# Fourier–Hyena encoder layer: later sines and tables in the opening, and part of the odd weights' and of token 512's arithmetic given to GpSimd

## The chip, the cores and the metric

The kernel runs on one core of a Trainium2 chip. The metric is the device time of one execution in microseconds (us), of which lower is better. The engines of the core are named as the profile names them: PE is TensorE's matmul, PEld its weight load, DVE is VectorE, ACT is ScalarE, POOL is GpSimd, and SP is SyncE, which here issues most of the DMA transfers. Each engine works through a queue of its own, in order; an instruction whose operands are not there yet holds up everything behind it on that engine.

## The reference

The layer is applied to two sequences of 1024 tokens and 1024 channels (`x_prompt` and `x_sample`). The Fourier branch, on which the change works, is the part below; the Hyena branch (long convolutions with filters that a small sine network makes), the gates and the output projection follow the same normalised input.

```python
def encoder_layer(x, g_pre, w_in, ...):
    xn = rmsnorm(x, g_pre)
    p = xn @ w_in
    fv, fg, hv, hg, mg = jnp.split(p, ...)
    fz = fv.astype(jnp.float32).reshape(B, L, F_GROUPS, F_GROUP_DIM)
    fz = jnp.fft.fftn(fz, axes=(1, 3), norm="ortho").real
    y_f = (fz * jax.nn.silu(fg)) @ w_fourier_out
...
def hyena_filters(L, w1, b1, f1, w2, b2, f2, w3, decay):
...
    h = jnp.sin(f1 * (z @ w1 + b1))
    h = jnp.sin(f2 * (h @ w2 + b2))
    h = (h @ w3).reshape(L, N_DIR, H_ORDER, H_WIDTH)
```

Everything is in float32. The kernel keeps that accuracy by splitting an operand into a rounded high part and the rest (`split`: a cast, then a subtraction of the cast from the source), and multiplying the parts separately.

## The kernel before

The program begins with `phase_fourier`, which runs the Fourier branch for the prompt (b = 0) and then for the sample (b = 1). The filter network, the projections, the convolutions and the output follow. The change touches the first 61 us, the opening of the prompt, before TensorE's work becomes continuous. In the opening these steps are written down in this order:

- `hidden(0)` (L271): the filter network's first layer. Two matmuls into `phd` (L295), then `sin_of` (L258 to L269) reduces the argument on DVE, and the nested function `sines` takes the sine on ACT (L301, with a table load of its own) and stores `d_h1` (L302). The result lies in the tile `hd_0`, which takes a buffer of the ring `eo`. `sines` is called so that it stands behind the last square of `norm` on ACT.
- `norm(0)` (L306): eight loads of x, 512 KB each (L320), a square with sum on ACT for each (L323), and for each four of them a chain of 11 small DVE operations (`rstd`, L241 to L252), which gives `rs`, and four diagonal matrices `dg` (L328).
- For each k of the eight channel blocks, `weights(..., k, True)` (L363) and `xtile(0, k, ...)` (L331). `weights` loads a block of the Fourier columns of the projection into `wfv` (L367, 260 KB, two buffers) and forms their even part (`wer`, an addition) and their odd part (`wor`, a subtraction), with two buffers each. Each is then split into a rounded part by ACT (`we0`, `wo0`, L171) and a second part (`we1`, `wo1`, L181). `xtile` transposes and normalises x by matmuls with `dg` into PSUM (`tpx`, L194, two buffers `T`), copies it out on ACT in two halves (`xg`, L347, two buffers), stores it to `d_x` on SP (L348), and forms sums and differences of mirrored tokens (`eo`, DVE, 2 of 128x512). These are split into `eh` (ACT, L171) and `el` (DVE, L181). Token 512 is split separately into `x5` (a cast, L173, and a subtraction, L181, of 128x2).
- For each k the matmuls `pfv` (L194) add up products of `eh`, `el` with `we`, `wo` for the first half of the columns. They are the last thing before `fourier_half`, whose first matmuls (`pse`) read the table `seq`.
- Constant tables: `seq` (2064 KB), `alt` (86 KB), `chan` (384 KB) and `chx` (256 KB) are loaded through POOL's queue (L538 to L541). Two small casts on POOL (L537) that read `rs` hold `seq` and `chan` back until the norm is done; `alt` and `chx` wait for nothing.

The instructions are written stage by stage, and a scheduler decides ahead of the run in which order each engine's queue holds them. `tc.issue_after(i)` keeps what is written under it behind instruction i in that order. A ring of two buffers (`xg`, `wfv`, `wer`, `wor`, `T`) means that round k+2 waits until all readers of round k are done; for `xg` the store to `d_x` is one of these readers. The second half of the columns (the call of `weights` with `first` False) has its odd part and its second part on POOL already.

Of the kernel before, what the change touches and what calls it, by code (L numbers as in the profile page):

```python
# [9 lines left out]
F32 = mybir.dt.float32  # L10
# [6 lines left out]
P = 128  # L17
D = 1024
L = 1024
# [142 lines left out]
class K:  # L162
# [5 lines left out]
    def split(self, h, l, src, eng="pool", heng="act"):  # L168
        nc = self.nc
        if heng == "act":  # L170
            self.rounded = nc.scalar.copy(h, src)  # L171
        else:
            nc.vector.tensor_copy(h, src)  # L173
        self.left = self.sub(eng, l, src, h)
# [96 lines left out]
    def hidden(self, layer, px, pf):  # L271

        nc, a = self.nc, self.a
        h = px.tile([P, L], F32, tag="eo", name=f"hd_{layer}", bufs=2)
        out = [h[:, 0:512], h[:, 512:1024]]
        z = px.tile([P, L], F32, tag="x", name="hd_z", bufs=3)
        if layer == 0:
# [5 lines left out]
            w, z = w[0:33], z[0:33]  # L283
            y, k = [[pf.tile([P, 512], F32, tag=f"{t}p{n}", name=f"s{t}", bufs=1 + (t == "p")) for n in range(2)]
                    for t in "qp"]
        else:
# [12 lines left out]
        def sines():  # L299
            for n in range(2):  # L300
                nc.scalar.activation(out[n], y[n], AF.Sin)  # L301
            nc.sync.dma_start(self.d_h if layer else self.d_h1, h)  # L302
        return sines
# [26 lines left out]
    def xtile(self, b, k, px, fo):  # L330
# [11 lines left out]
        for n in range(2):  # L342
# [4 lines left out]
            nc.scalar.activation(xg[:, 512 * n:512 * n + 512], tp, AF.Copy, scale=self.gpre[:, k:k + 1])  # L347
        nc.sync.dma_start(self.d_x[b][k], xg[:, 0:L])  # L348
        eo = px.tile([P, 2, 2, 256], F32, tag="eo", name="eo", bufs=2)
# [5 lines left out]
        x5 = fo["x5"][:, k]  # L355
        self.split(x5[:, b:b + 33:32], x5[:, 2 + b:35 + b:32], xg[:, 512:513].to_broadcast([P, 2]), "dve", "dve")

# [5 lines left out]
    def weights(self, pw, W, half, k, first):  # L363
# [6 lines left out]
        self.add("dve", we, w[:, :, 0], w[:, :, 1])  # L370
        self.sub("dve" if first else "pool", wo, w[:, :, 0, 0:128], w[:, :, 1, 0:128])
        for r, t in ((we, W[0]), (wo, W[1])):
            self.split(t[0][:, k], t[1][:, k], r.rearrange("p a b -> p (a b)"), "pool" if r is wo and not first else "dve", "act")

# [114 lines left out]
    def phase_fourier(self):  # L489
        tc, nc, a = self.tc, self.nc, self.a  # L490
        with ExitStack() as es:
# [5 lines left out]
            fo = {}  # L497
# [13 lines left out]
            for b in range(NB):  # L511
                fo["eh"] = pe.tile([P, 8, 2, 2, 256], F32R, tag="eh", name="eh")
                fo["el"] = pe.tile([P, 8, 2, 2, 256], F32R, tag="el", name="el")
                if b == 0:
                    sines = self.hidden(0, px, pf)
                with tc.issue_after(behind.ins) if b else ExitStack():
                    self.norm(b, px, pf)
                if b == 0:
                    with tc.issue_after(self.squared.ins):
                        sines()  # L520
                begun = {}
# [4 lines left out]
                for k in range(8):  # L526
                    if b == 0:
                        with tc.issue_after(self.scaled.ins):
                            self.weights(pw, W, 0, k, True)
                    self.xtile(b, k, px, fo)  # L530
                    for (e, m), p in begun.items():
                        self.pfv(p, e, m, k, W, fo)
                for half in ((0, 1), (1, 0))[b]:
                    if b + half == 0:
                        nc.sync.dma_start(self.vec, a["c_vec"])
                        for t in ("seq", "chan"):
                            nc.gpsimd.tensor_copy(fo[t][:, 0, 0:1], self.rs[:, 7:8])  # L537
                        nc.gpsimd.dma_start(fo["seq"], a["c_seq"])  # L538
                        nc.gpsimd.dma_start(fo["alt"], a["c_alt"])
                        nc.gpsimd.dma_start(fo["chan"], a["c_chan"])  # L540
                        nc.gpsimd.dma_start(fo["chx"].rearrange("p a b c -> p (a b c)"), a["c_chx"])  # L541
                    elif b + half != 2:
# [982 lines left out]
```

## Time and profile before

| | us |
|---|---|
| median of 3 runs | 2418.81 (2416.72 to 2419.53) |
| the profiled execution | 2420.15 |
| its span in the trace | 2418.3 |
| first transposes begin on PE | 16.19 |
| first `pfv` matmul begins | 27.65 |
| first `pse` matmul begins (end of the opening) | 60.83 |

All times in the trace count from the start of the span. The views used below are the page of the whole run, the list of waits (which engine's instruction stood idle, for which producer, in total, how often, and the longest), tables of busy time by stretch of time, the timeline (start, duration, engine, line, operation), and the lists for single lines and groups, which give the duration of one instruction and the time that a DMA transfer took from its issue to its landing. Of the DVE's work in the opening, the 16 `wor` and `wo` operations took 0.42 us each, and the casts and subtractions of `x5` mostly 0.16 us each.

### The profile page before, as it was taken

What the parts mean: (1) busy time and instruction counts of PE and PEld (TensorE: products, weight loads), DVE (VectorE), ACT (ScalarE), POOL (GpSimd) and SP (SyncE); (2) the same over time, 40 slices, a digit from 0 to 9 for tenths busy, and PEclk for the clock granted to TensorE, in tenths of its full rate; (3) what the DMA queues carried; (4) which work ended last, traced back from release to release, by engine and by line L of the source; (5) the groups of instructions that cost most, each with busy time, mean ns of one, the idle gap of its engine ahead of it and who ended that gap; (6) DMA issues with size and microseconds to landing.
All of it is one profiled execution on the core that took longest, in us unless ns stands there. A gap on an engine that the chain in (4) does not pass through costs nothing. (4 is left out here: it accounts for less than half of the span.)

```text
span 2418.3 us, 37119 instructions
## 1 busy us (share of the span) xinstructions
PE 2360.6 (98%) x13006; PEld 2050.7 (85%) x13006; DVE 1976.0 (82%) x3760; ACT 1147.7 (47%) x2140; POOL 447.5 (19%) x575
## 2 busy tenths in 40 slices
PE   6999899999999999999999999999999999999998
PEld 6998788888888888888888888888878888888886
DVE  7786888888737999899899999997666687777787
ACT  6546666666544444344222322333344475656543
POOL 1331111111123332221023454310000000101000
PEclk9999899999999999999999999999999999999999
DMA  7536688787778777666365666553546687888754
GB/s 277 187 127 220 179 222 222 202 225 215 202 219 254 221 223 209 192 177 200 126 194 191 210 218 205 187 179 123 205 158 230 210 298 256 267 270 230 222 159 154
DMA packets 265010, 499.63 MB, mean 207 GB/s; under 512 B 26662, under 2 KB 92423, under 8 KB 264568
## 3 DMA queue, kind: packets, MB, share of 16 engines
q1 hardware_dynamic: 220076, 380.53, 48.0%
q0 software_dynamic: 44560, 116.72, 19.0%
q8 instruction: 102, 1.67, 0.3%
q14 instruction: 84, 0.69, 0.1%
q10 hardware_dynamic: 188, 0.02, 0.0%
HBM read 333.59 MB, written 167.77 MB: 207 GB/s over the span
## 5 line engine op out<-in xcount | busy, mean ns | idle before, releaser
L194 PE MATMUL pin<-xh,wh 128*128 128x512 f32 x1024 | 401.2, 393 | 0.4 <-DMA wh<-d_w 0.4
L194 PE MATMUL pin<-xl,wh 128*128 128x512 f32 x1024 | 401.2, 392 | 0.0
L194 PE MATMUL pin<-xh,wl 128*128 128x512 f32 x1024 | 399.6, 392 | 0.0
L194 PE MATMUL pin<-xh,whl 128*128 128x512 f32 x896 | 292.4, 397 | 8.1 <-DMA whl<-in_w_in 4.5
L194 PEld LDWEIGHTS pin<-xh,wh 128*128 128x128 f32 x1024 | 192.8, 188 | 35.9 <-DMA wh<-d_w 0.8
L194 PEld LDWEIGHTS pin<-xh,wl 128*128 128x128 f32 x1024 | 192.7, 188 | 35.6 <-DMA wl<-in_w_in 0.2
L194 PEld LDWEIGHTS pin<-xl,wh 128*128 128x128 f32 x1024 | 192.7, 188 | 34.8
L194 PEld LDWEIGHTS pin<-xh,whl 128*128 128x128 f32 x896 | 168.3, 190 | 42.8 <-DMA whl<-in_w_in 5.2
L194 PE MATMUL pT<-cinv,yh 128*128 128x256 f32 x1024 | 192.9, 283 | 2.7 <-ACT yh L171 2.7
L194 PE MATMUL pin<-xl,whl 128*128 128x512 f32 x448 | 178.1, 398 | 0.0
L194 PEld LDWEIGHTS pT<-cinv,yh 128*128 128x128 f32 x1024 | 165.4, 191 | 12.9 <-ACT yh L171 3.2
L194 PE MATMUL pX<-bh,cfwd 128*128 128x256 f32 x768 | 159.3, 287 | 0.9 <-ACT bh L171 0.9
L181 DVE TENSOR_TENSOR t<-pX,k 128x1024 f32<-128x1024 f32 x128 | 155.7, 1216 | 3.9 <-PE pX L194 2.9
L171 ACT CAST yh<-y 128x512 fp32r<-128x512 f32 x128 | 79.3, 620 | 152.8 <-DVE y L181 113.1
L194 PE MATMUL pT<-cinv,yl 128*128 128x256 f32 x512 | 145.5, 284 | 0.0
L171 ACT CAST bh<-b 128x512 fp32r<-128x512 f32 x144 | 88.9, 619 | 98.3 <-DVE b L181 58.1
L194 PEld LDWEIGHTS pX<-bh,cfwd 128*128 128x128 f32 x768 | 125.8, 191 | 4.6 <-ACT bh L171 1.3
L181 POOL TENSOR_TENSOR draw<-draw 128x256 f32<-128x256 f32 x96 | 93.8, 977 | 112.1 <-DMA draw<-in_w_out 39.5
L181 DVE TENSOR_TENSOR bl<-b,bh 128x512 fp32r<-128x512 f32 x144 | 100.3, 703 | 11.5 <-ACT bh L171 11.4
L194 PE MATMUL pX<-bl,cfwd 128*128 128x256 f32 x384 | 109.5, 285 | 0.0
L181 DVE TENSOR_TENSOR yl<-y,yh 128x512 fp32r<-128x512 f32 x128 | 90.2, 705 | 16.9 <-ACT yh L171 16.5
L194 PEld LDWEIGHTS pT<-cinv,yl 128*128 128x128 f32 x512 | 98.2, 192 | 1.9
(368 smaller groups left out, 6030.0 us busy)
## 6 DMA issues: line engine op xcount, KB each, us to landing
k<-d_k SPq DMA_DIRECT2D x128, 512.0 KB, 4.6
wr<-in_w_in SPq DMA_DIRECT2D x136, 256.0 KB, 3.6
d_g<-gt SPq DMA_DIRECT2D x92, 256.0 KB, 3.3
d_k<-kt SPq DMA_DIRECT2D x128, 128.0 KB, 3.7
d_k<-kt SPq DMA_DIRECT2D x64, 256.0 KB, 3.6
fz<-d_g SPq DMA_DIRECT2D x64, 256.0 KB, 5.1
wl<-in_w_in POOLq DMA_DIRECT2D x56, 256.0 KB, 5.4
whl<-in_w_in POOLq DMA_DIRECT2D x56, 256.0 KB, 5.7
```

Of the source, the lines that this page charges most:

```text
L171: self.rounded = nc.scalar.copy(h, src)
L181: return e.tensor_tensor(out, a, b, op=op)
L194: return self.nc.tensor.matmul(out, lhsT, rhs, start=start, stop=stop, skip_group_check=shared)
```

## The change

Six things change, all of them in the opening of the prompt:

1. `split` can have its cast done by POOL. The `x5` parts of the prompt, 8 casts and 8 subtractions of 128x2, go from DVE to POOL.
2. The odd weight part `wor` and the second part `wo1` of the first half, 16 operations of 128x256, go from DVE to POOL.
3. `sines` of the first layer is called behind the `eh` cast of k = 2, instead of behind the last square. Its result lies in buffers of its own (a third set of the tag `p`) instead of a buffer of the ring `eo`.
4. `d_h1` is stored in two halves of 64 rows (128 KB each), where 128 rows were stored at once (512 KB). Only these 64 rows are read later.
5. The tables are loaded later. `seq` is divided into the columns of its two halves. The first half and `alt` are held back by a POOL cast that reads `el` of k = 3, the second half by one that reads `el` of k = 4, `chan` and `chx` by one that reads `el` of k = 5.
6. The first loads of x for the sample are issued behind the store of `d_x` for k = 4 as well.

```diff
@@ split
-            nc.vector.tensor_copy(h, src)
+            (nc.vector if heng == "dve" else nc.gpsimd).tensor_copy(h, src)
@@ hidden
-        h = px.tile([P, L], F32, tag="eo", name=f"hd_{layer}", bufs=2)
-        out = [h[:, 0:512], h[:, 512:1024]]
+        if layer:
+            h = px.tile([P, L], F32, tag="eo", name=f"hd_{layer}", bufs=2)
+            out = [h[:, 0:512], h[:, 512:1024]]
...
-            y, k = [[pf.tile([P, 512], F32, tag=f"{t}p{n}", name=f"s{t}", bufs=1 + (t == "p")) for n in range(2)]
-                    for t in "qp"]
+            y, k, out = [[pf.tile([P, 512], F32, tag=f"{t}p{n}", name=f"s{t}", bufs=1 + (t == "p")) for n in range(2)]
+                         for t in "qpp"]
...
                 nc.scalar.activation(out[n], y[n], AF.Sin)
-            nc.sync.dma_start(self.d_h if layer else self.d_h1, h)
+                if layer == 0:
+                    nc.sync.dma_start(self.d_h1[64:128, 512 * n:512 * n + 512], out[n][64:128])
+            if layer:
+                nc.sync.dma_start(self.d_h, h)
@@ xtile
-        self.split(x5[:, b:b + 33:32], x5[:, 2 + b:35 + b:32], xg[:, 512:513].to_broadcast([P, 2]), "dve", "dve")
+        mid = xg[:, 512:513].to_broadcast([P, 2])
+        self.split(x5[:, b:b + 33:32], x5[:, 2 + b:35 + b:32], mid, "dve" if b else "pool", "dve" if b else "pool")
@@ weights
-        self.sub("dve" if first else "pool", wo, w[:, :, 0, 0:128], w[:, :, 1, 0:128])
+        self.sub("pool", wo, w[:, :, 0, 0:128], w[:, :, 1, 0:128])
         for r, t in ((we, W[0]), (wo, W[1])):
-            self.split(t[0][:, k], t[1][:, k], r.rearrange("p a b -> p (a b)"), "pool" if r is wo and not first else "dve", "act")
+            self.split(t[0][:, k], t[1][:, k], r.rearrange("p a b -> p (a b)"), "pool" if r is wo else "dve", "act")
@@ phase_fourier
-                with tc.issue_after(behind.ins) if b else ExitStack():
+                with tc.issue_after(behind.ins) if b else ExitStack(), tc.issue_after(stored.ins) if b else ExitStack():
                     self.norm(b, px, pf)
-                if b == 0:
-                    with tc.issue_after(self.squared.ins):
-                        sines()
...
                     self.xtile(b, k, px, fo)
+                    if b == 0 and k == 2:
+                        with tc.issue_after(self.rounded.ins):
+                            sines()
+                    if b == 0 and k == 4:
+                        stored = self.stored
...
-                        for t in ("seq", "chan"):
-                            nc.gpsimd.tensor_copy(fo[t][:, 0, 0:1], self.rs[:, 7:8])
-                        nc.gpsimd.dma_start(fo["seq"], a["c_seq"])
-                        nc.gpsimd.dma_start(fo["alt"], a["c_alt"])
-                        nc.gpsimd.dma_start(fo["chan"], a["c_chan"])
-                        nc.gpsimd.dma_start(fo["chx"].rearrange("p a b c -> p (a b c)"), a["c_chx"])
+                        chx = fo["chx"].rearrange("p a b c -> p (a b c)")
+                        tables = [(3, fo["seq"][:, :, 0:1032], a["c_seq"][:, :, 0:1032]), (3, fo["alt"], a["c_alt"]),
+                                  (4, fo["seq"][:, :, 1032:2064], a["c_seq"][:, :, 1032:2064]),
+                                  (5, fo["chan"], a["c_chan"]), (5, chx, a["c_chx"])]
+                        for k, t, src in tables:
+                            nc.gpsimd.tensor_copy(t[:, 0, 0:1] if len(t.shape) > 2 else t[:, 0:1],
+                                                  fo["el"].bitcast(F32)[:, k, 0, 0, 0:1])
+                            nc.gpsimd.dma_start(t, src)
```

Three queues show what moves. Numbers at the ends of names tell the buffers of one ring apart; `xg0_1` is b = 0, k = 1.

The first is ACT's queue right behind the eighth square. Before it read:

```order
L301 ACT_TABLE_LOAD
L301 ACTIVATE hd_0_296<-sq_303 128x512
L301 ACTIVATE hd_0_296<-sq_304 128x512
L347 ACTIVATE xg0_0_417<-tpx_419,gpre_66 128x512
L171 CAST we0_397<-wer_409 128x260
L171 CAST wo0_399<-wor_410 128x256
L171 CAST we0_397<-wer_459 128x260
L171 CAST wo0_399<-wor_460 128x256
L347 ACTIVATE xg0_1_467<-tpx_469,gpre_66 128x512
L347 ACTIVATE xg0_0_417<-tpx_425,gpre_66 128x512
L347 ACTIVATE xg0_1_467<-tpx_475,gpre_66 128x512
L171 CAST eh_294<-eo_432 128x1024
```

The same place of the changed kernel, from the cast of the first odd weights (k = 0) to the first `eh`:

```order
L171 CAST wo0_397<-wor_408 128x256
L351 ACTIVATE xg0_0_415<-tpx_417,gpre_66 128x512
L171 CAST wo0_397<-wor_458 128x256
L171 CAST we0_395<-wer_407 128x260
L171 CAST we0_395<-wer_457 128x260
L351 ACTIVATE xg0_1_465<-tpx_467,gpre_66 128x512
L171 CAST we0_395<-wer_507 128x260
L171 CAST wo0_397<-wor_508 128x256
L351 ACTIVATE xg0_0_415<-tpx_423,gpre_66 128x512
L171 CAST we0_395<-wer_561 128x260
L171 CAST wo0_397<-wor_562 128x256
L351 ACTIVATE xg0_1_465<-tpx_473,gpre_66 128x512
```

The sines are gone from here, and the casts for k = 2 (`wer_507`, `wor_508`) and k = 3 (`wer_561`, `wor_562`) now stand ahead of the second halves of `xg` of k = 0 and k = 1.

The second is POOL's queue behind the two small loads at the program's start. Before:

```order
L539 DMA alt<-in_c_alt 128x172
L541 DMA chx<-in_c_chx 128x512
L341 MEMSET xg_0_417 128x2
L341 MEMSET xg_1_467 128x2
L537 CAST seq<-rs_326 128x1
L537 CAST chan<-rs_326 128x1
L538 DMA seq<-in_c_seq 128x4128
L540 DMA chan<-in_c_chan 128x768
L341 MEMSET xg_2_517 128x2
```

In the changed kernel (`wfv_405` to `wfv_659` are the weights of k = 0 to 5):

```order
L181 TENSOR_TENSOR wor_408<-wfv_405 128x256
L345 MEMSET xg0_1_465 128x2
L181 TENSOR_TENSOR wor_458<-wfv_455 128x256
L181 TENSOR_TENSOR wo1_398<-wor_408,wo0_397 128x256
L181 TENSOR_TENSOR wo1_398<-wor_458,wo0_397 128x256
L181 TENSOR_TENSOR wor_508<-wfv_505 128x256
L181 TENSOR_TENSOR wor_562<-wfv_559 128x256
L181 TENSOR_TENSOR wo1_398<-wor_508,wo0_397 128x256
L173 CAST x5_278<-xg0_0_415 128x2
L181 TENSOR_TENSOR x5_278<-xg0_0_415,x5_278 128x2
L181 TENSOR_TENSOR wo1_398<-wor_562,wo0_397 128x256
L181 TENSOR_TENSOR wor_612<-wfv_609 128x256
```

The four table loads have left this place; the weights' arithmetic, and token 512's, fill it.

The third is SP's queue behind the small constants. Before:

```order
L302 DMA d_h1_76<-hd_0_296 128x1024
L367 DMA wfv_507<-in_w_fv 128x520
L367 DMA wfv_557<-in_w_fv 128x520
L348 DMA d_x0_0_77<-xg0_0_417 128x1024
L348 DMA d_x0_1_78<-xg0_1_467 128x1024
L367 DMA wfv_607<-in_w_fv 128x520
L367 DMA wfv_657<-in_w_fv 128x520
L348 DMA d_x0_2_79<-xg0_2_517 128x1024
```

In the changed kernel:

```order
L372 DMA wfv_505<-in_w_fv 128x520
L372 DMA wfv_559<-in_w_fv 128x520
L372 DMA wfv_609<-in_w_fv 128x520
L372 DMA wfv_659<-in_w_fv 128x520
L352 DMA d_x0_0_77<-xg0_0_415 128x1024
L352 DMA d_x0_1_78<-xg0_1_465 128x1024
L372 DMA wfv_709<-in_w_fv 128x520
L372 DMA wfv_759<-in_w_fv 128x520
```

The loads of the weights for k = 4 and k = 5 have moved ahead of the stores of `xg` of k = 0 and k = 1, and the store of `d_h1` has gone behind.

From about 61 us on, the queues hold the same order as before up to about 290 us; in the filter and projection stages that follow, up to about 600 us, neighbouring instructions are exchanged here and there, and behind that the order is again the same.

More of the change, by code (lines that the diff above doesn't have):

```diff
@@ L347, in xtile @@
             nc.scalar.activation(xg[:, 512 * n:512 * n + 512], tp, AF.Copy, scale=self.gpre[:, k:k + 1])
-        nc.sync.dma_start(self.d_x[b][k], xg[:, 0:L])
+        self.stored = nc.sync.dma_start(self.d_x[b][k], xg[:, 0:L])
         eo = px.tile([P, 2, 2, 256], F32, tag="eo", name="eo", bufs=2)
```

## The prediction

> **What bounds the kernel now.** I read the page first, then the waits of the first 70 us, then the busy times by stretch, and last the single instructions of the opening. The page says who sets the time:
>
> ```profile
> span 2418.3 us, 37119 instructions
> PE 2360.6 (98%) x13006; PEld 2050.7 (85%) x13006; DVE 1976.0 (82%) x3760; ACT 1147.7 (47%) x2140; POOL 447.5 (19%) x575
> ```
>
> PE is idle for 2418.3 - 2360.6 = 57.7 us of the whole span by this count. The change takes no work from PE, so it can gain only idle time of PE, and only in the opening, since everything behind it begins when the opening's matmuls are done. The waits of the first 70 us (engine, tile and line that waited, what for, us in total, times, longest) show which idle time that is:
>
> ```profile
> PE tpx L194 <- DVE dg L328: 10.9, 2, 8.9
> ACT xg L347 <- DMA d_x<-xg: 2.3, 1, 2.3
> PE tpx L194 <- ACT xg L347: 2.5, 2, 1.3
> DVE wer L181 <- DMA wfv<-in_w_fv: 1.7, 1, 1.7
> PE pfv L194 <- DVE el L181: 2.0, 2, 1.3
> PE pfv L194 <- ACT eh L171: 0.4, 1, 0.4
> ```
>
> And the stretches (us, its length, then busy time of PE, PEld, DVE, ACT, POOL with the instruction counts, PE's granted clock, DMA share, GB/s):
>
> ```profile
> 0.00:16.20 16.20, 3.75 (x5) 1.17 (x5) 10.34 (x33) 9.10 (x14) 2.61 (x9) 1.00 0.89 324
> 20.30:27.60 7.30, 7.30 (x39) 7.28 (x40) 5.67 (x17) 4.87 (x9) 1.06 (x2) 1.00 0.87 315
> 27.60:35.30 7.70, 5.05 (x40) 4.51 (x38) 4.92 (x11) 2.55 (x5) 0.10 (x1) 1.00 1.00 335
> 35.30:43.20 7.90, 7.88 (x65) 7.67 (x66) 7.29 (x19) 6.90 (x13) 0.20 (x2) 1.00 0.73 255
> 43.20:52.50 9.30, 8.13 (x70) 7.93 (x69) 9.30 (x22) 6.09 (x11) 2.48 (x4) 1.00 0.61 212
> 52.50:60.80 8.30, 7.17 (x57) 6.66 (x55) 6.19 (x13) 3.26 (x6) 0.58 (x2) 1.00 0.78 242
> ```
>
> From 20.3 to 60.8 us PE is busy 7.30 + 5.05 + 7.88 + 8.13 + 7.17 = 35.53 of 40.50 us, so **4.97 us** are idle. They have two limits. From 27.6 to 35.3 us, where 2.65 are idle, no engine is full, but the DMA share is 1.00: ACT cannot write `xg` because the store of the buffer's former contents is not out, and DVE waits for `wfv`. From 43.2 us on DVE is the limit (9.30 of 9.30); there 1.17 + 1.13 = 2.30 us are idle. The remaining 0.02 is in the stretch between.
>
> **Change by change.** First the second `dg`, at which PE idles before 20.3 us, and what stands on DVE and PE around it:
>
> ```profile
> 20.29 7.61 PE L194 MATMUL tpx<-dg,x 128*128 128x128 f32 x40 [2.02 <-DVE dg L328]
> 19.94 0.88 DVE L328 TENSOR_SCALAR dg<-ident,rs 128x128 f32<-128x128 f32 x4
> 20.74 0.41 DVE L181 TENSOR_TENSOR wer<-wfv 128x260 f32<-128x260 f32 x1
> alt<-in_c_alt POOLq DMA_DIRECT2D x1, 86.0 KB, 7.3
> chx<-in_c_chx POOLq DMA_DIRECT2D x1, 256.0 KB, 8.8
> ```
>
> `alt` and `chx`, 342 KB, share the DMA engines with the loads of x. At the 324 GB/s of the first stretch they take 350 thousand bytes / 324 GB/s = 1.1 us. Without them the last x, its square and the second `dg` come up to 1.1 us earlier. The first `dg` does not move, because DVE is held there by the argument reduction of the filter. Against this stands that `wor` and `wo1` of k = 0 and 1, four POOL operations, now run while DVE works through the norm's chain. What this does to DVE is bounded from two places where both engines work side by side:
>
> ```profile
> 50.22 2.83 POOL L181 TENSOR_TENSOR wor<-wfv 128x256 f32<-128x256 f32 x2 [2.86 <-DVE wo L181]
> 50.04 0.44 DVE L181 TENSOR_TENSOR we<-wer,we 128x260 fp32r<-128x260 f32 x1
> 50.38 0.43 DVE L181 TENSOR_TENSOR wo<-wor,wo 128x256 fp32r<-128x256 f32 x1
> 50.71 0.63 DVE L181 TENSOR_TENSOR x<-xg,x 128x2 fp32r<-128x2 f32 x1
> L181 DVE TENSOR_TENSOR x<-xg,x x8: 149/163/626, 26.4 to 57.3; 128x2 fp32r<-128x2 f32 x8
> 69.45 1.62 POOL L181 TENSOR_TENSOR wo<-wor,wo 128x256 fp32r<-128x256 f32 x2 [16.36 <-ACT wo L171]
> 71.03 1.61 POOL L181 TENSOR_TENSOR wor<-wfv 128x256 f32<-128x256 f32 x2
> 71.27 0.86 DVE L181 TENSOR_TENSOR wer<-wfv 128x260 f32<-128x260 f32 x1
> ```
>
> A POOL operation of this size takes 0.81 (69.45, 71.03) to 1.42 us (50.22, where DVE was full). The DVE operation that meets it takes longer: 0.63 instead of the median 0.16 (+0.47), and 0.86 instead of the 0.43 of its neighbours (+0.43). So each meeting costs DVE about **0.45 us**. The four in the norm's chain cost DVE 0 to 1.8. The term is therefore -1.1 to +0.7 (1.8 - 1.1); I take **0**, near the middle, since the first two of the four may find DVE between two chains.
>
> The rule behind such rows is in the Trainium skill, "SBUF — State Buffer", section "SBUF: two separate sides": VectorE with two SBUF inputs and GpSimd share one pair of ports as an exclusive lock, and the loser waits for the other's whole instruction. The rows agree that one waits, but not for how long: +0.45 on DVE is about half of POOL's 0.81. By the page's full instruction the 16 weight operations would cost DVE up to 16 x 0.81 = 13 us, an estimate.
>
> Next the crowded stretch, with the tables and the two kinds of transfers that wait beside them (KB, median us from issue to landing; then the spread for `d_x` and for `wfv`):
>
> ```profile
> seq<-in_c_seq POOLq DMA_DIRECT2D x1, 2064.0 KB, 9.7
> chan<-in_c_chan POOLq DMA_DIRECT2D x1, 384.0 KB, 12.1
> d_h<-hd SPq DMA_DIRECT2D x1, 512.0 KB, 2.7
> DMA to landing us min/median/max: 3.1/6.1/9.5
> DMA to landing us min/median/max: 2.8/6.4/11.3
> ```
>
> `seq` and `chan`, 2448 KB, are 7.5 us of DMA at 335 GB/s, and they lie right ahead of `wfv` for k = 2 and 3 and of the first two stores of `xg`. With them gone until k = 3, a store lands after some 3.1 us instead of 9.5, and `wfv` after some 2.8. Both waits of this stretch then lose their cause, which is **-2.65**. What is late next is ACT, which in the new order stands behind POOL:
>
> ```profile
> 17.74 1.28 ACT L301 ACT_TABLE_LOAD   x1
> 19.04 1.15 ACT L301 ACTIVATE hd<-sq 128x512 f32<-128x512 f32 x2
> 21.52 0.40 ACT L171 CAST wo<-wor 128x256 fp32r<-128x256 f32 x1
> 24.21 0.69 ACT L347 ACTIVATE xg<-tpx,gpre 128x512 f32<-128x512 f32 x1 [0.53 <-PE tpx L194]
> 26.50 1.03 ACT L171 CAST eh<-eo 128x1024 fp32r<-128x1024 f32 x1
> L181 DVE TENSOR_TENSOR eo<-xg x16: 679/694/702, 25.0 to 56.7; 128x512 f32<-128x512 f32 x16
> ```
>
> The second half of `xg` of k = 0, before at 24.21, now follows the cast of `wo0` for k = 2. `wfv` for k = 2 can be issued when `wer` of k = 0 has read its buffer (20.74 + 0.41 = 21.15) and lands 2.8 later, at 23.95; POOL's `wor` takes 0.9 (nearer to 0.81 than to 1.42, as DVE is not full here: 5.67 of 7.30), and the cast 0.40. `xg` starts at 25.25, and after its 0.69 and two `eo` of 0.69 the first `eh` at 27.3 instead of 26.50. The first `pfv` is **+0.8** late; the bounds are 0, if the norm ends 1.1 earlier, and +1.3, with 1.42 for POOL. Behind the waiting ACT instruction stand the second halves of `xg` of k = 0 and 1, for which the PSUM buffers of the next transposes wait, but PE's 40 passes to 27.9 us cover that. SP too has a new order: `wfv` for k = 4 and 5 stand ahead of the first two stores of `d_x`, and wait there for POOL's `wor` of k = 2 and 3, until about 26. The stores then land near 26 + 3.1 = 29.1, well before 35.3, up to which the stretch waited for them.
>
> The sines, 1.28 + 1.15 = 2.43 us, leave ACT before 20.2, where PE waited for `dg`, not for ACT, which gives 0. They come back behind `eh` of k = 2. ACT is busy 2.55 of 7.70 and 6.90 of 7.90 there; the sum with them, 11.9 of 15.6, fits. I take 0; at worst, with all of them in the fuller stretch, 2.43 - 1.00 = +1.4. Their store shrinks from 512 to 256 KB and leaves the crowd, which is in the -2.65.
>
> Now DVE. What it loses has these rows:
>
> ```profile
> L181 DVE TENSOR_TENSOR wo<-wor,wo 128x256 fp32r<-128x256 f32 x8 | 3.4, 422 | 0.0
> L181 DVE TENSOR_TENSOR wor<-wfv 128x256 f32<-128x256 f32 x8 | 3.4, 421 | 0.0
> ```
>
> Starts are 0.34 apart (50.04, 50.38), 0.10 less than one lasts, so the 16 are worth 16 x 0.34 = 5.4 us, and the 16 of `x5` at 0.16 - 0.10 each 1.0: **6.4 us** of DVE's 5.67 + 4.92 + 7.29 + 9.30 + 6.19 = 33.37. What comes back is 0.45 for each of the 32 POOL operations that meets a DVE operation: 0 if none does, 14.4 if all do. So DVE gains 6.4 or loses 8.0. I take half of them, 7.2, as DVE is busy about 80% of this stretch but many of POOL's operations are a few elements wide. That leaves DVE at +0.8, and the 2.30 idle us from 43.2 on stay: **0** (-2.30 to the rival below).
>
> The tables, 2.8 MB with `alt` and `chx`, now come between some 41 and 52 us, where the DMA share was 0.61 to 0.78. The first matmul that reads `seq` starts at the end of the opening, so they are there in time: 0, up to +2.65 if they crowd out the stores of `xg` as before. Behind 61 us the order is the same or exchanges neighbours where PE hardly waits; 0, give or take 1.
>
> **The sum**: 0 - 2.65 + 0.8 + 0 + 0 + 0 = -1.85 us. Against the profiled execution (2420.15, which is 1.3 above the median shown) that is 2418.3; against the median of 2418.81 it is **2417.0**.
>
> **The rivals.** (a) *Both limits really go.* POOL's operations fall into DVE's pauses and nothing new waits: 4.97 + 1.1 = -6.1, **2412.7**. For it: DVE's idle is 7.1 us of 40.5. Against it: DVE is full where POOL would have to get in. (b) *The tables crowd the later stores instead.* The -2.65 is paid again at k = 4 to 6: -1.85 + 2.65 = +0.8, **2419.6**. The change then does in effect nothing but move the wait. For it: the DMA share of 0.78 at the end; against it: they come in three pieces, and no other 2 MB transfer is in front. (c) *DVE is slowed more than relieved*, at k = 2 to 7, where PE's `pfv` follow `el`. With all 32 meeting, DVE needs 33.4 + 8.0 = 41.4 us plus waits of its own that stay. Of the 7.1 us idle the waits for `wfv` (1.7) and a part of those for `xg` go; I keep 2.5. That is 43.9 against 40.5, +3.4, with +0.7 at the norm and +1.3 at ACT, the upper ends of these terms: +5.4, **2424.2**. It decides from (7.1 - 2.5 + 6.4) / 32 = 0.34 us of DVE for each POOL operation, that is, when three in four meet a DVE operation. Against it: half of the 32 are only two elements wide. By the full lock of the Trainium skill's page this rival would be the likely one; its 13 us stand against +0.45 an operation in the rows.
>
> **Chances.** The forecast (small gain) 0.51, (a) 0.17, (b) 0.18, (c) 0.14. A range that holds 8 in 10 takes in (b) and reaches to the prices of (a) and (c), as all three costs (meeting, table crowd, ACT behind POOL) are unmeasured: 2412.0 to 2424.5. About 0.2%, here 4.8 us, is what a measurement of this kernel can tell from no change. Only (a) with all its parts gets beyond it on the fast side, and only (c) on the slow side: faster 0.16, same 0.70, slower 0.14.
>
> **What would show it.** In the profile of the changed kernel: the stretch from 27.6 to 35.3 has no wait of ACT for `d_x` and none of DVE for `wfv`; the first `pfv` begins near 28.4; POOL's 128x256 operations last 0.8 to 1.4 us and DVE's neighbours of them 0.86; DVE stays nearly full in the middle of the opening; the first `pse` begins near 59 instead of 60.8. The prediction is wrong if PE idles less than 1 us between 30 us and the first `pse` (then a), if ACT waits for `d_x` at k = 4 to 7 (then b), if `pfv` waits for `el` or `eh` by more than 4 us in sum (then c), or if PE's clock warms up at another time, which no row of mine prices.

## The result, and the profile after

The changed kernel takes 2427.73 us (median of 12 runs, 2423.58 to 2432.10) where the kernel before took 2421.68 in the same comparison (12 runs). The ratio is **1.0025, with a 95% interval of 1.0016 to 1.0033**: 0.25% slower, 6 us. The prediction was 2417.0, a gain of 1.8 us, within a range of 2412.0 to 2424.5; the kernel got slower, and the time lies above that range.

The page of the changed kernel (a profiled execution of 2427.98 us):

```profile
span 2425.9 us, 37125 instructions
PE 2364.2 (97%) x13006; PEld 2053.3 (85%) x13006; DVE 1978.8 (82%) x3728; ACT 1147.4 (47%) x2140; POOL 472.1 (19%) x611
```

The span is 7.6 us longer. PE's timeline tells where (start, duration, work, in brackets the idle time ahead of it and what ended it):

```profile
17.86 2.33 PE L194 MATMUL tpx<-dg,x 128*128 128x128 f32 x8 [10.52 <-DVE dg L332]
21.30 5.25 PE L194 MATMUL tpx<-dg,x 128*128 128x128 f32 x24 [1.11 <-DVE dg L332]
27.52 2.35 PE L194 MATMUL tpx<-dg,x 128*128 128x128 f32 x16 [0.96 <-ACT xg L351]
30.40 1.23 PE L194 MATMUL pfv<-we,eh 128*128 128x260 f32 x8 [0.53 <-ACT eh L171]
33.87 2.05 PE L194 MATMUL tpx<-dg,x 128*128 128x128 f32 x16 [1.78 <-ACT xg L351]
39.73 1.16 PE L194 MATMUL tpx<-dg,x 128*128 128x128 f32 x8 [0.77 <-ACT xg L351]
44.32 1.16 PE L194 MATMUL tpx<-dg,x 128*128 128x128 f32 x8 [1.28 <-ACT xg L351]
60.95 2.10 PE L194 MATMUL pfv<-we,eh 128*128 128x260 f32 x8 [3.88 <-ACT eh L171]
68.19 0.48 PE L194 MATMUL pse<-seq,ee 128*128 128x258 f32 x2
```

Before the change PE had these waits behind that of 2.02 us for the second `dg`:

```profile
32.97 0.75 PE L194 MATMUL pfv<-we,el 128*128 128x260 f32 x4 [1.31 <-DVE el L181]
35.28 3.23 PE L194 MATMUL tpx<-dg,x 128*128 128x128 f32 x24 [1.34 <-ACT xg L347]
46.08 2.05 PE L194 MATMUL tpx<-dg,x 128*128 128x128 f32 x16 [1.17 <-ACT xg L347]
54.93 0.75 PE L194 MATMUL pfv<-we,el 128*128 128x260 f32 x4 [0.70 <-DVE el L181]
58.49 1.23 PE L194 MATMUL pfv<-we,eh 128*128 128x260 f32 x8 [0.43 <-ACT eh L171]
```

The first `pse` begins at 68.19 instead of 60.83, so 7.36 of the 7.6 us are lost in the opening. They fall into three parts. The first transposes begin at 17.86 instead of 16.19 (+1.67). PE's waits between 20 us and the first `pse` add up to 10.31 us in the timeline, 6.97 before (+3.34). And PE works more slowly for the same passes (+2.35, the rest of the 50.33 us from the first transposes to the first `pse`, 44.64 before). Eight `pfv` passes at 60.95 take 2.10 us; eight at 30.40 take 1.23. The 36 passes from 60.95 to the first `pse` take 7.24 us; before, the last 18 took 2.34 (58.49 to 60.83), so the slow passes are nearly all there. The table of stretches shows them beside PE's clock (columns as before):

```profile
28.50:35.30 6.80, 4.46 (x34) 3.89 (x33) 6.71 (x10) 4.59 (x9) 5.71 (x10) 1.00 0.83 278
35.30:43.20 7.90, 6.97 (x58) 6.58 (x56) 7.07 (x9) 5.42 (x10) 6.63 (x11) 1.00 0.46 167
43.20:50.00 6.80, 5.68 (x49) 5.68 (x50) 5.32 (x8) 4.99 (x9) 3.98 (x9) 1.00 0.85 254
50.00:57.10 7.10, 7.07 (x62) 6.87 (x60) 4.42 (x6) 2.54 (x4) 5.43 (x12) 1.00 0.98 291
57.10:61.00 3.90, 0.05 (x1) 0.05 (x1) 0.07 (x1) 1.72 (x3) 0.10 (x1) 0.91 1.11 405
61.00:68.20 7.20, 7.20 (x37) 7.10 (x37) 3.66 (x5) 2.02 (x4) 1.18 (x2) 0.57 0.84 310
```

From 57.1 to 61.0 us nearly everything stands still while the DMA share is above 1.00, and behind that PE's granted clock is 0.57. What stood still is read from the waits of the first 75 us:

```profile
ACT xg L351 <- DMA d_x<-xg: 5.4, 1, 5.4
PE tpx L194 <- ACT xg L351: 4.8, 4, 1.8
PE pfv L194 <- ACT eh L171: 4.4, 2, 3.9
ACT wo L171 <- POOL wor L181: 3.7, 2, 2.5
DVE wer L181 <- DMA wfv<-in_w_fv: 1.8, 2, 1.6
```

PE no longer waits for DVE's `el` at all (2.0 us before). It waits for ACT. And ACT waits for POOL, and once, for 5.4 us, for a store, here on ACT, on POOL's queue and on SP's:

```profile
59.28 0.69 ACT L351 ACTIVATE xg<-tpx,gpre 128x512 f32<-128x512 f32 x1 [5.41 <-DMA d_x<-xg]
59.87 1.03 ACT L171 CAST eh<-eo 128x1024 fp32r<-128x1024 f32 x1
...
49.13 0.75 POOL L550 DMA_DIRECT2D seq<-in_c_seq  x1
...
50.14 4.09 SPq L352 DMA_DIRECT2D d_x<-xg  x2
```

The `xg` at 59.28 is the first half of k = 7. Its buffer is that of k = 5, and the store of k = 5 went out at 50.14, 1.0 us behind the first half of `seq`; it landed 9.0 us after its issue, where the prediction had reckoned with 3.1 for the first stores. `eh` of k = 6 stands behind that `xg` on ACT, and PE's `pfv` behind `eh`.

### The profile page after: what moved, and what is told of

It reads as the page before. It is cut to its first block, busy times and chain, and to the rows that moved or that the text cites. A ratio compares the mean times of both kernels' runs of the same rounds, so it can differ in the third digit from the quotient of the medians.

```text
span 2425.9 us, 37125 instructions
## 1 busy us (share of the span) xinstructions
PE 2364.2 (97%) x13006; PEld 2053.3 (85%) x13006; DVE 1978.8 (82%) x3728; ACT 1147.4 (47%) x2140; POOL 472.1 (19%) x611
## 3 DMA queue, kind: packets, MB, share of 16 engines
q8 instruction: 102, 1.67, 0.3%
## 5 line engine op out<-in xcount | busy, mean ns | idle before, releaser
L194 PEld LDWEIGHTS pin<-xh,wh 128*128 128x128 f32 x1024 | 193.1, 189 | 35.6 <-DMA wh<-d_w 0.4
L194 PEld LDWEIGHTS pin<-xl,whl 128*128 128x128 f32 x448 | 85.3, 190 | 16.7
```

Source lines behind the costliest of these rows:

```text
L194: return self.nc.tensor.matmul(out, lhsT, rhs, start=start, stop=stop, skip_group_check=shared)
```

## The experiments

The kernels were compared with the kernel before on the same chip. The time at which DVE can begin differs between executions of any kernel (the start of its first instruction, which waits for the small load `ident`, lay between 5.40 and 7.05 us in these profiles, whatever the kernel), and all of the opening moves with it. So the length of the opening is counted from the first transposes to the first `pse`, in one profile each. Behind the opening the profiles scatter as much as the openings differ: that of e2_tables_alone is the slowest of its ten executions (2425.97 us; the other nine took 2412.46 to 2415.45), though its opening is the shortest of all. The ratios rest on 5 to 12 executions of each kernel, not on the profiled one.

| kernel | ratio to before (95%) | opening, us | PE's longest wait in it |
|---|---|---|---|
| before | | 44.64 | 2.02 |
| changed | 1.0025 (1.0016 to 1.0033) | 50.33 | 3.88 |
| e1_tables_early | 1.0024 (1.0012 to 1.0036) | 48.56 | 2.23 |
| e2_tables_alone | **0.9975** (0.9963 to 0.9988) | 39.38 | 1.48 |
| e3_eh_first | 1.0028 (1.0017 to 1.0038) | 47.31 | 4.06 |
| e4_pool_alone | 1.0013 (1.0000 to 1.0025) | 47.77 | 3.51 |
| e5_no_pool | 0.9995 (0.9986 to 1.0005) | 42.86 | 1.77 |
| e6_x5_pool | 0.9985 (0.9971 to 0.9999) | 42.35 | 1.8 |
| e7_weights_pool | 1.0000 (0.9989 to 1.0011) | 42.88 | 1.09 |
| e8_first_two_dve | 0.9998 (0.9988 to 1.0007) | 44.78 | 2.54 |
| e9_sines_early | 1.0018 (1.0008 to 1.0028) | 49.38 | 4.52 |
| e10_tables_x5 | 0.9985 (0.9974 to 0.9997) | 39.41 | 1.60 |
| e11_tables_123 | 1.0033 (1.0021 to 1.0045) | 51.49 | 4.49 |
| e12_sines_alone | 1.0002 (0.9991 to 1.0013) | 46.33 | 2.69 |
| e13_tables_456 | 1.0003 (0.9994 to 1.0012) | 43.63 | 1.26 |
| e14_fill | 1.0055 (1.0039 to 1.0072) | 52.94 | 3.25 |

**Which part costs.** The first four set two theories against each other: the late tables block a store (T), or POOL's work slows the whole opening (P).

e1_tables_early, in the changed kernel:

```diff
-                        tables = [(3, fo["seq"][:, :, 0:1032], ...), (3, fo["alt"], ...), (4, ...), (5, ...), (5, ...)]
-                        for k, t, src in tables:
...
+                        for t in ("seq", "chan"):
+                            nc.gpsimd.tensor_copy(fo[t][:, 0, 0:1], self.rs[:, 7:8])
+                        nc.gpsimd.dma_start(fo["seq"], a["c_seq"])
...
```

> The changed kernel with its tables loaded as before the change (seq and chan behind the norm, alt and chx at once); all else as changed. Theory T (the late tables hold up the store of xg of k = 5, ACT stands on that store with eh of k = 6 behind it, PE idles 3.9 us and goes on at a lower clock): the wait before the last pfv and the clock of 0.57 behind it are gone, 6 us less than the changed kernel, and up to 2.65 us for the old crowd at 28 to 35 us come back: first pse between 61.8 and 64.5 us instead of 68.2, time within 0.15% of before. Theory P (POOL's operations slow DVE through the whole opening, the rest follows from that): first pse stays above 66 us, time 0.2% or more above before.

e2_tables_alone is the reverse of this edit in the kernel before, and nothing else.

> The kernel before with the later tables alone. Theory T: the store of xg of k = 5 or 6 takes 7 to 9 us and PE waits 2 us or more before the last pfv, at a lower clock behind it; the 2.65 us at 28 to 35 us go; first pse between 60 and 66 us. Theory P: the 2.65 go and nothing comes, first pse near 58.2, time 0.1% below before.

e3_eh_first, in the changed kernel (`eh6` is the cast of `eh` for k = 6):

```diff
+            with self.tc.issue_after(self.eh6.ins) if b == 0 and k == 7 else ExitStack():
-            nc.scalar.activation(xg[:, 512 * n:512 * n + 512], tp, AF.Copy, scale=self.gpre[:, k:k + 1])
+                nc.scalar.activation(xg[:, 512 * n:512 * n + 512], tp, AF.Copy, scale=self.gpre[:, k:k + 1])
```

> The changed kernel with one pair of ACT instructions exchanged: eh of k = 6 stands ahead of the first half of xg of k = 7, which waits for the store. Theory T: pfv of k = 6 (18 passes, 2.2 us at full clock) fills more than half of the 3.9 us, what is left is under 2 us, the clock stays at 1.00: first pse 63 to 65 us, 3.5 to 5 us less than the changed kernel. Theory P: no difference beyond the scatter, first pse 67 to 69.

e4_pool_alone, in the kernel before:

```diff
-        self.sub("dve" if first else "pool", wo, ...)
+        self.sub("pool", wo, ...)
...
-                       "pool" if r is wo and not first else "dve", "act")
+                       "pool" if r is wo else "dve", "act")
...
-        self.split(x5..., "dve", "dve")
+        self.split(x5..., "dve" if b else "pool", "dve" if b else "pool")
```

> The kernel before with POOL's new work alone (wor and wo1 of the first half, x5); tables and sines as before. Theory T: 0 to 2 us later than before at the first pse (60.8 to 63), time within 0.1%. Theory P: 4 to 7 us later, time 0.2% or more above before.

e1 speaks against T as the only cause: without the late tables the changed kernel is as slow as with them, though the wait of 3.9 us is gone. e2 speaks against T more strongly: alone, the later tables make the kernel **0.25% faster**, more than the 0.1% that P expected of them, and its opening is 5.3 us shorter. e4 gives P half of what it wanted: POOL's work alone costs 0.13%, with an interval that just touches zero, and 3.1 us of opening. In e3 the exchange on ACT let the `pfv` of k = 6 run ahead (opening 47.31 instead of 50.33), but the wait came back in front of k = 7 (4.06), with the slow passes behind it, and the total did not move: a miss. Neither theory was enough: -6, +3 and something that makes +6 of them together.

**POOL's parts.** The next four take the changed kernel and give work back to DVE: all of it (e5), the weights (e6), `x5` (e7), and the weights of k = 0 and 1 only (e8):

```diff
# e6_x5_pool; e5_no_pool has this and the one below
-        self.sub("pool", wo, ...)
+        self.sub("dve" if first else "pool", wo, ...)
-                       "pool" if r is wo else "dve", "act")
+                       "pool" if r is wo and not first else "dve", "act")
# e7_weights_pool
-        self.split(x5..., "dve" if b else "pool", "dve" if b else "pool")
+        self.split(x5..., "dve", "dve")
# e8_first_two_dve
-        self.sub("pool", wo, ...)
+        self.sub("dve" if first and k < 2 else "pool", wo, ...)
-                       "pool" if r is wo else "dve", "act")
+                       "pool" if r is wo and not (first and k < 2) else "dve", "act")
```

> The changed kernel with all POOL arithmetic of the first half (wor, wo1, x5) back on DVE; later tables and later sines stay. Theory P (POOL's operations cost more than they relieve: they hold DVE, and ACT's queue stands on them): first pse 56.5 to 58 us, 0.2 to 0.3% less than before, as with the later tables alone. Theory S (the later sines or the order made around them share in the loss): first pse 59 to 62, within 0.1% of before.

> The changed kernel with wor and wo1 back on DVE, x5 alone on POOL. If the 16 small operations are the costly half (each held DVE by up to 0.47 us, and they postpone the tables in POOL's queue): first pse 61 us or more, time at or above before. If the 128x256 operations are: first pse 57 to 59 us, 0.15 to 0.3% less than before.

> The changed kernel with x5 back on DVE, wor and wo1 alone on POOL. If the 128x256 operations are the costly half, as ACT's casts of wo wait for wor and xg stands behind them: first pse 64 to 68 us, 0.15 to 0.3% more than before. If the small operations are: first pse 57 to 60 us, at or below before.

> The changed kernel with wor and wo1 of k = 0 and 1 on DVE, those of k = 2 to 7 on POOL. If the four operations beside the norm's chain matter (dg took 0.45 instead of 0.28 us each): the four dg and rs take their old time, the first transposes start 1 us earlier, and about that much of the total is gained, 0.04%. If the loss lies at k = 2 to 7: no difference beyond the scatter, first pse 66 to 69 us.

In all four, most or all of the 6 us are gone. e5 came out as its theory S has it. e6 points to the 128x256 operations as the costly half, but e7, which keeps just those on POOL, came out between its two expectations (first `pse` at 61.60). `x5` alone on POOL costs nothing (e6 against e5, 0.9985 and 0.9995 with overlapping intervals). The weights alone are at 1.0000. e8 is the surprise: four operations fewer on POOL were expected to give 0.04% and gave 0.27%. Such a step is not the price of four operations of 0.7 us; a small lateness must tip something over.

e5 shows another cost. It differs from e2 by the later sines with their halved store, and by the sixth change (the first x of the sample is loaded at 42.46 us, in e2 at 50.28), which no run has alone. From the first `eh` on, ACT's timeline is the same in both, shifted by 0.2 us, up to one place. e2_tables_alone on ACT:

```profile
35.76 1.04 ACT L171 CAST eh<-eo 128x1024 fp32r<-128x1024 f32 x1
36.70 0.69 ACT L347 ACTIVATE xg<-tpx,gpre 128x512 f32<-128x512 f32 x1
```

e5_no_pool at the same place, and DVE behind it:

```profile
35.55 1.04 ACT L171 CAST eh<-eo 128x1024 fp32r<-128x1024 f32 x1
36.61 1.28 ACT L302 ACT_TABLE_LOAD   x1
37.90 1.15 ACT L302 ACTIVATE sp<-sq 128x512 f32<-128x512 f32 x2
38.96 0.67 ACT L351 ACTIVATE xg<-tpx,gpre 128x512 f32<-128x512 f32 x1
...
39.73 1.30 DVE L181 TENSOR_TENSOR eo<-xg 128x512 f32<-128x512 f32 x2 [1.23 <-ACT xg L351]
```

The sines stand ahead of the second half of `xg` of k = 3, which then runs 2.5 us later against the `eh` in front of it, and DVE waits for it. The opening of e5 is 3.5 us longer than that of e2. Of these, 1.95 are waits of PE behind the sines that e2 does not have (0.94 for that `xg`, then 0.72 for `el` and 0.29 for `eh`); most of the rest lies ahead of the sines, at the first transposes.

**What tips over.** e9 takes the sines back to their old place in the changed kernel, e10 adds `x5` on POOL to e2, e11 loads the tables two blocks earlier than the change does, and e12 puts the later sines alone into the kernel before:

```diff
# e9_sines_early (changed kernel)
+                if b == 0:
+                    with tc.issue_after(self.squared.ins):
+                        sines()
...
-                    if b == 0 and k == 2:
-                        with tc.issue_after(self.rounded.ins):
-                            sines()
# e10_tables_x5 (e2)
-        self.split(x5..., "dve", "dve")
+        self.split(x5..., "dve" if b else "pool", "dve" if b else "pool")
# e11_tables_123 (changed kernel): el of k = 1, 2, 3
-                        tables = [(3, seq first half), (3, alt), (4, seq second half), (5, chan), (5, chx)]
+                        tables = [(1, seq first half), (1, alt), (2, seq second half), (3, chan), (3, chx)]
# e12_sines_alone (kernel before): the edit of e9 backwards, with the sines' own buffers and the halved store
```

> The changed kernel with the sines (2.43 us of ACT) behind the last square again; later tables and POOL's work stay. Theory S (behind eh of k = 2 the sines stand ahead of the second half of xg of k = 3, for which DVE and PE wait; ahead of the first xg they cost nothing): the time between the first transposes and the first pse falls from 50.3 by 2.4 us or more, and with the pipeline earlier by that much the store of xg of k = 5 goes out ahead of seq, which takes the wait of 3.9 and the low clock away too: 42 to 45 us, total 0.1% below to 0.1% above before. Without the second effect: near 48, total 0.15% above before.

> The kernel before with the later tables and with x5 on POOL; sines and weights as before. If the parts add up: 0.25% below before from the tables, and 0 to 0.1% more from x5: 2411 to 2415 us on the scale where before has 2420, first transposes to first pse 38 to 40 us.

> The changed kernel with its tables held back by el of k = 1, 2 and 3 instead of 3, 4 and 5. Theory R (the wait of 3.9 us and the low clock come from the first half of seq getting onto the DMA queues just ahead of the store of xg of k = 5): seq is out by about 45 us, the store takes under 5 us, the wait before the last pfv is under 1.5 us, the clock stays at 1.00, first transposes to first pse 44 to 46 us instead of 50.3, total about 0.2% less than the changed kernel. If R is wrong and the lateness is POOL's alone: 48 to 51 us, no difference.

> The kernel before with the later sines alone (and the halved store). Theory S: the sines delay the second half of xg of k = 3 by 2.4 us less what ACT stands idle there: 1 to 2.5 us longer from the first transposes to the first pse (44.6 before), total 0.05 to 0.1% above before. As the prediction had it: no difference.

e10 adds up in the opening (39.41), and with 0.9985 it is as fast as e2 within the intervals. e12's opening is 1.7 us longer, but 1.16 of that are 24 transposes at a lower clock from 35.83 us on (4.39 us instead of 3.23), ahead of the sines, which begin at 39.72; its total can't be told from before. So it doesn't price the sines. e9 took off 1 us and kept the long wait. e11 refuted its theory as it was put: with earlier tables the wait is 4.49 us. But the profiles gave the order that all have in common. In the changed kernel, e3, e9 and e11 the store of `xg` of k = 5 is issued (at 49.0 to 50.6 us) behind the first half of `seq`; it lands 9.0 to 9.5 us later, and in those four PE waits 3.9 to 4.5 us near the end. In e2, e5, e6, e7, e8 and e10 the store is ahead of it (at 40.8 to 47.3 us), and there is no such wait. Earlier tables are then worse, and later ones should be better:

```diff
# e13_tables_456 (changed kernel)
-                        tables = [(3, seq first half), (3, alt), (4, seq second half), (5, chan), (5, chx)]
+                        tables = [(4, seq first half), (4, alt), (5, seq second half), (6, chan), (6, chx)]
# e14_fill (changed kernel)
-            for q in range(4):
+            for q in [0, 1, 2, 3] * (4 if b == 0 and k == 7 and n == 1 else 1):
```

> The changed kernel with its tables held back by el of k = 4, 5 and 6 instead of 3, 4 and 5. Theory R2 (the wait of 3.9 us before the last pfv arises when the store of xg of k = 5 is issued behind the first half of seq; loading the tables later puts the store ahead): the store of k = 5 lands within 5 us, no wait above 1.5 us follows from 50 us on, the clock stays at 1.00, first transposes to first pse 43 to 46 us instead of 50.3, total 0 to 0.1% above before. If the load as such is the cause, whatever the order: a wait of 2 us or more stays, at k = 6 or 7 or for seq, 48 us or more, total 0.2% above before.

> The changed kernel with the transposes of the second half of k = 7 done four times over into the same PSUM tile (24 more passes, 2.8 us), at the place where PE is about to wait. Theory C (PE's clock falls to 0.57 because PE stood idle for 3.9 us): the idle time falls to 1 us or so, the clock stays at 1.00 between 61 and 68 us, the 36 passes of the last two pfv take 4.7 instead of 7.1 us, first pse near 66 instead of 68.2, although PE does more. If the clock has another cause: first pse at 68 or later.

e13 came out as R2 has it, in the total too (1.0003). SP, POOL and PE of e13_tables_456:

```profile
48.45 3.88 SPq L352 DMA_DIRECT2D d_x<-xg  x2
...
50.41 0.74 POOL L550 DMA_DIRECT2D seq<-in_c_seq  x1
...
58.52 1.21 PE L194 MATMUL pfv<-we,eh 128*128 128x260 f32 x8 [1.14 <-ACT eh L171]
...
60.84 0.48 PE L194 MATMUL pse<-seq,ee 128*128 128x258 f32 x2
```

The store of k = 5 is out 2.0 us ahead of `seq`, the wait before the last `pfv` is 1.14 us, the eight passes take 1.21, and nothing of the change has been taken away. The store lands 3.3 us after its issue instead of 9.0. So the order of one store and one table load is worth some 0.2% in this kernel (`chan` and `chx` came a block later too; the opening waits for neither). The x load of the sample stands ahead of that store in both kernels (46.54 and 44.65 us), so it is not what held it up.

e14 missed its time: the scheduler spread the added passes over two places, PE waited at both, and with 24 passes more the kernel is slower. But its two waits tell of the clock, in one execution:

```profile
60.84 1.24 PE L194 MATMUL pfv<-we,eh 128*128 128x260 f32 x8 [2.55 <-ACT eh L171]
...
67.19 2.10 PE L194 MATMUL pfv<-we,eh 128*128 128x260 f32 x8 [3.25 <-ACT eh L171]
```

The same eight passes take 1.24 us behind 2.55 us of idling, and 2.10 behind 3.25. So the slower clock is a price of the idle time, and filling part of it kept the clock up. The traffic is no rival here: the DMA share was 1.13 in the first wait too (58.0 to 60.84 us). How much idle time it takes is not settled by the length of one wait. In e12_sines_alone two shorter ones, with 1 us of work between, brought a granted clock of 0.50 (35.83 to 38.50 us):

```profile
34.56 0.75 PE L194 MATMUL pfv<-we,el 128*128 128x260 f32 x4 [2.69 <-DVE el L181]
35.83 4.39 PE L194 MATMUL tpx<-dg,x 128*128 128x128 f32 x24 [0.29 <-ACT xg L351]
```

## Why the prediction was wrong

Point by point, by its own terms:

- **The norm, taken as 0, was near it where the prediction priced it, but the first `dg` moved.** The transposes behind the second `dg` begin at 21.30 instead of 20.29; 0.85 of that is the start of DVE, which differs between executions and is not the change's, so 0.16 is left. The prediction also said that the first `dg` does not move. The first transposes came 1.67 later, 0.82 without the start of DVE, and this is POOL beside DVE. DVE and POOL of the changed kernel:

```profile
16.51 0.56 DVE L252 SCALAR_TENSOR_TENSOR rs<-rs_t,rs 128x4 f32<-128x4 f32 x1
17.10 1.78 DVE L332 TENSOR_SCALAR dg<-ident,rs 128x128 f32<-128x128 f32 x4
...
16.41 0.63 POOL L181 TENSOR_TENSOR wor<-wfv 128x256 f32<-128x256 f32 x1 [0.65 <-DMA wfv<-in_w_fv]
```

  One of the chain's operations took 0.56 instead of 0.16, and the four `dg` 1.78 instead of 0.87. That is within the bound given for DVE (0 to 1.8). Before, DVE had stood idle for 1.03 us ahead of the second chain; that time took up the delay.

- **The -2.65 for the crowd was right in kind and too small.** In the changed kernel neither ACT waits for `d_x` nor DVE for `wfv` from 27.6 to 35.3 us, as forecast. e2 has the term alone: the opening is 5.3 us shorter. The waits fall from 6.97 to 2.94 us, among them all of the 2.30 us from 43 us on; one of 1.48 for `el` stays at 31.70. The prediction left those 2.30, since DVE was full there. In e2 DVE is full from 41 to 48 us as well (7.00 of 7.00), and PE waits for nothing. A full engine is not yet what the next one waits for, if its results come early enough. That in the kernel before the crowd had made them late is argued, not shown.
- **ACT behind POOL, taken as +0.8**, was +1.1 up to the first `pfv` (12.54 us after the first transposes, 11.46 before). It did not end there: 1.78, 0.77 and 1.28 us of PE's waits for `xg` followed, which the prediction did not have (the last behind the sines).
- **The sines, taken as 0, cost about 2 us where they were seen**: the 1.95 between e2 and e5, in one profile each, with the sixth change in it. e12, alone, shows no loss that can be laid to them. The step failed because it asked whether ACT had room in the stretch (11.9 of 15.6 us), and not what stood behind the sines in ACT's queue.
- **DVE, taken as +0.8, came out near it, at about -0.4.** In the stretch from 12 to 66 us the groups that stay on DVE took 29.6 us before, all with those that leave 40.0; in the changed kernel the ones that stay are:

```profile
L181 DVE TENSOR_TENSOR eo<-xg 128x512 f32<-128x512 f32 x16 | 12.3, 810 | 1.4 <-ACT xg L351 0.8 <-ACT we L171 0.5
L181 DVE TENSOR_TENSOR el<-eo,eh 128x1024 fp32r<-128x1024 f32 x8 | 10.2, 1275 | 8.9 <-ACT eh L171 8.9
L181 DVE TENSOR_TENSOR wer<-wfv 128x260 f32<-128x260 f32 x10 | 5.7, 578 | 1.9 <-DMA wfv<-in_w_fv 1.8
L181 DVE TENSOR_TENSOR we<-wer,we 128x260 fp32r<-128x260 f32 x8 | 4.2, 532 | 0.3 <-ACT we L171 0.2
L332 DVE TENSOR_SCALAR dg<-ident,rs 128x128 f32<-128x128 f32 x8 | 3.2, 454 | 0.1
```

  Together 35.6. The meetings with POOL cost 6.0 us (35.6 - 29.6), 0.19 for each of the 32 operations; the prediction had 7.2. The 10.4 that left overstate the relief, as these durations overlap; by the spacing of starts, as the prediction counted, it is 6.4, and 6.4 - 6.0 leaves 0.4. So rival (c) did not decide: DVE has 8.9 us to spare behind `eh`, and a relief would be worth nothing, because PE waits for ACT. The Trainium skill, "SBUF — State Buffer", section "SBUF: two separate sides", says that the loser of the shared ports waits for the winner's whole instruction. The trace agrees that a DVE operation is held up: the one above grew by 0.40 us beside a POOL operation of 0.63. The 0.19 is an average over operations of which half are 128x2 and not all met one of DVE's, so it does not test whether a whole instruction is waited for.
- **The tables, taken as 0, cost 3.9 us of waiting and most of the 2.35 of slower passes.** This is the step that failed for good, and rival (b) is its name: the late tables crowd a later store. The prediction had them between some 41 and 52 us, at a DMA share of 0.61 to 0.78; they were issued from 49.13 to 56.24, and the share rose to 1.11. It priced the rival at 2.65, the waits that the same crowd had caused before, and gave it 0.18. Its own sign for (b) appeared, ACT's wait for `d_x` at k = 7. So did the sign for (c), 4.4 us of `pfv` waiting for `eh`, but 3.88 of them stand behind that store. It missed two things. Here, ACT has `eh` of k = 6 behind the waiting `xg`, so that PE runs dry altogether. And a wait of that length lowers the clock behind it. The Trainium skill has the second in "TensorE: Matmul & The Clock Gate", section "Part 1: The HAM clock gate (the "warmup" mystery)": after about 3.4 us without work the clock is halved, in windows that run freely. The trace agrees with the halving (0.50 from 60.95 to 67.00 us) and in e14 roughly with the time: 3.25 us brought the 2.10 us passes, 2.55 did not. e12 shows that less in one piece can do it: 2.69 and 0.29.

Neither the tables, POOL's work, nor the sines do this alone. In e2 the tables come late and the pipeline is early, so that the store is ahead of `seq`. With POOL's waits and the sines the pipeline is late at k = 5: counted from the first transposes, the store goes out after 32.3 us, in e8 after 30.4, in e2 after 26.0, and it falls behind. Taking back part of POOL's work (e5 to e8), or moving the tables on by one block (e13), puts the store ahead again. The sines' return alone (e9) was not enough. e1, with early tables, has no such wait and still 1.0024: there the old crowd of 28 to 37 us (2.23 and 1.19 us of PE's waits) and POOL's and the sines' lateness add up; 24 transposes behind these waits took 5.49 us, where the kernel before has 3.23 for 24. How much each of the three has in that is not settled.

The collision is not the whole loss. e13 has no collision and all of the change, with the tables one block later, and is still no faster than before (1.0003), where the tables alone gain 0.25% (e2). So POOL's work and the sines together cost about as much as the tables gain, some 0.28%, and the collision adds some 0.22% on top. That is far more than the 0.8 us that the prediction had for POOL's work and the 0 for the sines, and no run tells their shares safely apart.

The version to keep is e2_tables_alone: the kernel before with the later tables and nothing else, 0.25% faster than before (2414.45 against 2420.43 us) and 0.5% faster than the change as made.

## What to carry to other kernels

A transfer that is moved out of one crowd joins another: look up which store or load its queue places come to stand in front of, which ring waits for that one, and what stands behind the waiting instruction on its engine. An edit that makes a pipeline a few us later is not priced by its own length if a deadline of order (here one store ahead of one table) lies within those few us. And an engine's spare time is no cover for work put in front of a critical instruction; the queue's order decides, not the share.

## What the runs showed of the hardware

- PE's clock: in these openings every wait of 3.25 us or more behind the first transposes (changed, e3, e4, e9, e11, e14) was followed by passes at little more than half speed, such as 2.10 instead of 1.23 us for eight, for about 3 us in e14 and about 6 in the changed kernel, where 36 passes took 7.24 us instead of twice 2.34. Two waits shortly after each other did it too, with 1 us of work between: 2.23 and 1.19 us in e1, 2.69 and 0.29 in e12. Single ones of 2.54 (e8) and 2.55 us (e14) did not.
- The granted clock does not show every slow stretch. Behind the 8.89 us of idling ahead of the first transposes it reads 1.00, yet a transposing pass took 421 ns there (16 to 18.3 us of the kernel before) and 275 from 35.28 us on; the weight loads took 333 and 192.
- One execution's start is not that of another: the small load `ident` let DVE begin at 5.40 to 7.05 us, whatever the kernel, so that one profile's 1 to 1.5 us in the first 17 us prove nothing.
- POOL's subtraction of 128x256 took 0.63 to 1.14 us where the changed kernel's rows show a single one, and two in a row 2.40 us beside a busy DVE (at 37.04 us); DVE does one in 0.42.
